# A Trainium2 expert stage: 64-row second blocks straight from the raw weights, a second output tensor for the last six blocks, and the final norm of all rows ahead of them

## The chip, the cores and the metric

The kernel runs on one core of a Trainium2 chip. The metric is the device time of the kernel in microseconds (us). Engines are named as in the profile: PE (TensorE) multiplies matrices, DVE (VectorE) and ACT (ScalarE) work on tiles, POOL (GpSimd) works on tiles and issues the indirect DMAs, SP (SyncE) issues most of the other DMAs.

## What is computed

A decoder block over S = 2048 rows of D = 1024 numbers, all in fp32: a norm, a projection, two attention mixers, a mixture of experts, a final norm. The change touches the last two. Cut to these, the reference is:

```python
# x: [2048, 1024] after the mixers; h = rms_norm(x, g)
grp = argmax(h @ w_group + b_group)              # one of 4 groups per row
top_v, top_i = top_k(e_logits_of_the_group, 2)   # 2 of its 8 experts
weight = p_grp * softmax(top_v)
# for each of the 4096 (row, expert) pairs:
y = (silu(h_row @ w_gate_e[e]) * (h_row @ w_up_e[e])) @ w_down_e[e]   # 1024 -> 256 -> 1024
x[row] += weight * y
out = rms_norm(x, norm_final_g)
```

There are 32 experts. How many rows each gets is known at run time only; with the reference's inputs it is 82 to 209 rows.

## The kernel before

One Python program writes the instructions of PE, DVE, ACT and POOL in an order that a planner (`Weave`) fixes beforehand: each piece of work is a generator that yields a time at which it can go on, each operation books a cost on its engine (`W.op`), and the piece that is ready first is written next. The engines then run their streams in that order and wait on semaphores. So an operation that waits holds up everything written behind it on its engine. SP's DMAs stand in one queue, in the order in which they were written, and at most eight of them are under way.

**Before the experts.** `route_setup` writes zero-weight entries into the four list tensors: 32 DMAs of 128 KB from the tile `padv`, on SP (L1407). They stand in the middle of the projection: on SP behind and ahead of them are the stores of q (L440), and behind these the loads of the next columns of the weights (`fraw`, L290). ACT evicts q from PSUM (L432) into tiles that the stores must have read before they are used again, and splits each weight column into a high and a low part (`apart`, L174 on ACT, L180 on DVE or POOL) for products in three matmuls (`mm3`, L187 to L189).

**Slots.** The experts are put in order of their row counts (experts 0 and 1 come first in any case). The 20 with the most rows get two blocks of 128 rows, the other 12 one: 52 slots, in the order of the list `SLOTS`; what is beyond is done by a loop at the end (L2254), which has nothing to do with these inputs. `lists` builds on DVE and PE (L2074) the table that says which row numbers belong to which slot. Then six generators run: `load` and `chunk` bring an expert's weights in six chunks of 512 KB, four of gate and up (L1915) and two of down (L1917), into a ring of four buffers `raw3`, and split them; a buffer is given back after its split. `fetch` gathers the slot's rows from `h2` (L1970, POOL, indirect). `turn` transposes them (L2108, eight transposes) and splits them. `enter` does gate and up (24 matmuls of 128x512), `act` silu and the product, `leave` the transposes of the result (L2162), its split, and down (12 matmuls), whose result is scaled on DVE and ACT (L2188, L2191) and added to the rows of `x2` in memory by an indirect store (`scatter`, L1977, POOL).

**The end.** `rest` first computes on DVE a table of what is left for the loop (L2217 to L2252, a dozen steps of up to 1x1024), reads its count (L2253), runs the loop, and then loads the 16 tiles of `x2` (L2305, SP), squares and sums each (L2311, ACT), computes the inverse roots in small DVE operations (L2313, `rsqrt`), scales (L2317, DVE) and stores (L2319, on ACT's queue).

## Time and profile before

| | before |
|---|---|
| median of three runs | 2665.09 us (2662.35 to 2671.33) |
| the profiled execution: its own time | 2665.63 us |
| its span in the trace | 2663.9 us |
| PE busy | 2469.3 us, 93% |
| DVE, ACT, POOL busy | 1470.3, 1070.2, 1169.7 us |
| DMA | 430.70 MB, mean 162 GB/s |
| expert stage, its slots | from about 2100 to 2610 us |

All rows of the trace are of that one execution, so its span and own time are what a sum is made against; the runs around it differ by a few microseconds. Busy shares are means over the whole span: the page's 93% hides that the stages have different limits, and the stretch at hand has to be read by itself. In the chain of waits each row is a piece of work that ended last at that point; what is not in the chain costs nothing as long as it stays out of it.

### The profile page before, as it was taken

To read this page: it belongs to the slowest core of one execution; us is meant where nothing else is said; L and a number is where in the kernel's file an instruction comes from. 1 tells how busy PE (TensorE), PEld (TensorE's weight loads), DVE (VectorE), ACT (ScalarE), POOL (GpSimd) and SP (SyncE) were. 2 spreads that over 40 slices of the span, in tenths; PEclk is the share of its full clock that TensorE was granted. 3 is DMA by queue.
4 is the path that set the end of the run, shared out by engine and by line. 5 is a ranking of instruction groups with operands and counts; after the bars stand their busy time and mean duration, and the time that the engine had idled before them with its cause. 6 is when DMAs were issued, how large, how long until landed. Compare 5 with 4: busy or idle time off the path is not lost.

```text
span 2663.9 us, 38518 instructions
## 1 busy us (share of the span) xinstructions
PE 2469.3 (93%) x13504; PEld 1928.7 (72%) x13504; DVE 1470.3 (55%) x3338; ACT 1070.2 (40%) x1674; POOL 1169.7 (44%) x931
## 2 busy tenths in 40 slices
PE   6999998989899899999999998999999899999991
PEld 5898886767566566677666664899888688888871
DVE  7402114757477666637776672422465566766666
ACT  5311113545333334344333333423332466666653
POOL 1012112323145556664566677444432356666650
PEclk9999998999999999999999998999999999999995
DMA  8613648676732242245322212865643479998877
GB/s 297 215 52 99 184 123 206 177 204 188 175 80 74 60 123 63 65 113 162 107 65 67 60 48 56 271 185 183 208 147 139 150 239 296 287 280 267 271 216 265
DMA packets 274682, 430.70 MB, mean 162 GB/s; under 512 B 52493, under 2 KB 184087, under 8 KB 270901
## 3 DMA queue, kind: packets, MB, share of 16 engines
q1 hardware_dynamic: 246967, 369.43, 46.0%
q0 software_dynamic: 16000, 33.63, 5.8%
q10 hardware_dynamic: 11520, 25.17, 2.5%
q8 instruction: 107, 1.75, 0.3%
q14 instruction: 88, 0.72, 0.1%
HBM read 317.18 MB, written 131.89 MB: 169 GB/s over the span
## 4 chain that ended last, share of the span: by engine, by line
PE 80%; DVE 7%; DMA 6%; POOL 3%; issue 2%; ACT 2%; SPq 1%; ACTq 0%; POOLq 0%; DVEq 0%
PE bank L321 21%; PE bank L187 10%; PE bank L189 10%; PE bank L188 10%; PE bank L1053 7%; PE bank L1001 4%; PE bank L1041 3%; PE bank L1044 3%; POOL zs L1062 2%; PE bank L1070 2%; PE bank L2108 2%; PE bank L1043 1%; PE bank L1029 1%; DMA qa<-q 1%; DMA gb<-gate 1%
## 5 line engine op out<-in xcount | busy, mean ns | idle before, releaser
L1046 ACT ACTIVATE p<-bank 128x512 f32<-128x512 f32 x458 | 266.2, 597 | 432.0 <-PE bank L1044 404.7
L180 POOL TENSOR_TENSOR fwl<-fraw,fwh 128x1024 fp32r<-128x1024 f32 x54 | 130.0, 2408 | 527.3 <-ACT fwh L174 497.9
L1062 POOL TENSOR_TENSOR zs<-zs,p 128x512 f32<-128x512 f32 x229 | 298.2, 1302 | 29.0 <-ACT p L1046 10.0
L1080 DVE RECIPROCAL rz<-bank 128x256 f32<-128x256 f32 x126 | 219.7, 1749 | 64.7 <-PE bank L1070 64.4
L321 PE MATMUL bank<-fhh,fwh 128*128 128x512 f32 x616 | 247.5, 402 | 4.1 <-ACT fwh L174 4.1
L321 PE MATMUL bank<-fhh,fwl 128*128 128x512 f32 x616 | 247.1, 401 | 1.7 <-POOL fwl L180 1.7
L321 PE MATMUL bank<-fhl,fwh 128*128 128x512 f32 x616 | 246.4, 400 | 0.0
L1053 PE MATMUL bank<-p,v 128*64 128x256 f32 x1704 | 234.5, 416 | 3.2 <-ACT p L1046 3.0
L174 ACT CAST wh<-raw 128x1024 fp32r<-128x1024 f32 x192 | 199.6, 1052 | 34.6 <-DMA raw<-in_w_gu_e_dram 22.7
L180 DVE TENSOR_TENSOR wl<-raw,wh 128x1024 fp32r<-128x1024 f32 x123 | 178.3, 1455 | 45.1 <-ACT wh L174 42.4
L180 POOL TENSOR_TENSOR wl<-raw,wh 128x1024 fp32r<-128x1024 f32 x69 | 167.3, 2425 | 81.7 <-ACT wh L174 81.2
L1044 PE MATMUL bank<-q,ka 128*128 128x512 f32 x426 | 199.6, 468 | 0.0
L1053 PEld LDWEIGHTS bank<-p,v 128*64 128x64 f32 x1704 | 124.7, 148 | 83.2 <-issue 22.7
L187 PE MATMUL bank<-wh,oh 128*128 128x512 f32 x416 | 172.4, 415 | 0.0
L1004 DVE TENSOR_REDUCE mx<-bank 128x1 f32<-128x512 f32 x192 | 128.2, 687 | 75.2 <-PE bank L1001 74.7
L1001 PE MATMUL bank<-kb,qa 96*128 96x512 f32 (+3 forms) x448 | 155.6, 378 | 9.3 <-DMA kb<-k 8.6
L189 PE MATMUL bank<-wh,ol 128*128 128x512 f32 x416 | 164.0, 394 | 0.0
L188 PE MATMUL bank<-wl,oh 128*128 128x512 f32 x416 | 163.3, 393 | 0.0
L1062 POOL TENSOR_TENSOR zs<-p 128x512 f32<-128x512 f32 x86 | 111.2, 1294 | 90.0 <-ACT p L1046 71.9
L1084 POOL TENSOR_TENSOR rz<-rz,gb 128x256 f32<-128x256 f32 x96 | 72.7, 758 | 175.8 <-DVE rz L1080 150.7
L1041 PE MATMUL bank<-qa,kb 97*128 97x512 f32 x362 | 148.7, 411 | 0.8 <-ACT qa L1031 0.7
L321 PEld LDWEIGHTS bank<-fhh,fwh 128*128 128x128 f32 x616 | 118.3, 192 | 30.9 <-ACT fwh L174 4.9
(490 smaller groups left out, 6091.5 us busy)
## 6 DMA issues: line engine op xcount, KB each, us to landing
raw<-in_w_gu_e_dram SPq DMA_DIRECT2D x128, 512.0 KB
fraw<-in_w_cols_dram SPq DMA_DIRECT2D x77, 512.0 KB
raw<-in_w_down_e_dram SPq DMA_DIRECT2D x64, 512.0 KB
xt<-in_x_dram SPq DMA_DIRECT2D x32, 512.0 KB
sg<-fo ACTq DMA_DIRECT2D x64, 256.0 KB
q<-q SPq DMA_DIRECT2D x64, 256.0 KB
sg<-sg SPq DMA_DIRECT2D x64, 256.0 KB
gb<-gate SPq DMA_DIRECT2D x64, 192.0 KB
```

The lines of the kernel that those rows point to most:

```text
L180: e.tensor_tensor(out=lo, in0=src, in1=hi.bitcast(F32), op=ALU.subtract)
L187: mm(out, lhsT=wh, rhs=xh, start=first, stop=False, **kw)
L188: mm(out, lhsT=wh, rhs=xl, start=False, stop=False, **kw)
L189: mm(out, lhsT=wl, rhs=xh, start=False, stop=last, **kw)
L321: K.T.matmul(ps, lhsT=w[:, k, :], rhs=self.H[ch][x][f][:, k % 4], start=k == 0 and j == 0, stop=k == 7 and j == 2)
L1001: T.matmul(ps[:, :w], lhsT=q1[0:rows, h, :], rhs=kb[0:rows, a:a + w], start=True, stop=True)
L1041: T.matmul(ps, lhsT=kb, rhs=q1, start=True, stop=False)
L1044: T.matmul(ps, lhsT=ka, rhs=q2, start=False, stop=True)
L1046: A.activation(p, ps, AF.Exp)
L1053: T.matmul(u[hp * 64:hp * 64 + 64, 0], lhsT=v, rhs=p[:, 2 * hp:2 * hp + 2, :], start=first, stop=last, skip_group_check=True)
L1062: e.tensor_tensor(out=out, in0=a, in1=b, op=ALU.add)
L1080: V.reciprocal(r, z)
```

## The change

**Half blocks.** Of the 20 experts with two blocks, the 15 in places 5 to 19 of the order now have a second block of at most 64 rows, a half block. Its rows are gathered as 64 rows, transposed into 64 columns and not split: ACT copies them, and the matmuls take fp32 on both sides, the weights straight from the raw chunks. 16 matmuls of 64x256 for gate and up write two groups of 64 columns into the two halves of a PSUM tile's partitions, 4 of 64x512 do down, each set in one unbroken piece (`enter_half`, `leave_half`). The result goes out in 128 pieces of 2 KB (`scatter_half`). The raw gate chunks of these experts go to a ring of their own (`fx`, four buffers `xf`), the two down chunks to `raw3`; all are given back when both their split and the half block have used them. The order of the experts is now in pairs, one other expert and one with a half block; the half block is done before the full one, but for the last expert.

**Table.** The steps of the table of what is left are a generator `table`, started as soon as the lists are there.

**z.** A second tensor `z` is zeroed by 16 DMAs behind the pads of the lists. The last six slots (`LATE`) add into z instead of x2.

**Final norm.** `finals` loads x2 once the other slots have been added, two tiles at a time, into buffers of `fx` and `raw3`, norms them and stores them (on SP's queue now). `once_more` then treats the rows of each of the six late slots: it gathers them from x2 and from z (POOL), adds (DVE), norms, and writes them to `out` by an indirect store; this comes after all 16 tiles have been stored.

**Setup.** `lists` has 16 more matmuls and two more DVE operations, `moe_setup` sets its table by 104 memsets instead of 16 and eight iotas.

```diff
+        zv = sc["z"].rearrange("(a p) (b n) -> a p b n", p=128, n=256)
+        for a in range(16):
+            nc.sync.dma_start(zv[a], pad[:, None, :].to_broadcast([128, 4, 256]))
...
-TWOS, ONES = 20, 12
-
-
+HALF = 64
+FULL, TWOS = 5, 20
+_halves, _others = list(range(FULL, TWOS)), list(range(2, FULL)) + list(range(TWOS, NE))
 ORDER = [(0, 2), (1, 2)]
-for _g in range(6):
-    ORDER += [(2 + 3 * _g, 2), (20 + 2 * _g, 1), (3 + 3 * _g, 2), (21 + 2 * _g, 1), (4 + 3 * _g, 2)]
+for _h, _o in zip(_halves, _others):
+    ORDER += [(_o, 2 if _o < FULL else 1), (_h, 2)]
 SLOTS = [(0, 0, 0), (1, 1, 0), (0, 0, 1), (1, 1, 1)]
-SLOTS += [(n, r, b) for n, (r, c) in enumerate(ORDER) for b in range(c) if n > 1]
+for _n, (_r, _c) in list(enumerate(ORDER))[2:]:
+    SLOTS += [(_n, _r, _b) for _b in ((1, 0) if FULL <= _r < TWOS - 1 else range(_c))]
 NS = len(SLOTS)
 
+LATE = 6
...
+        self.fx = K.keep("mf", bufs=4)
+        self.fR = Ring(4)
...
+                if c < 4 and is_half(r):
+                    self.fR.take()
+                    raw = self.fx.tile([128, 1024], F32, name="xf")
+                else:
+                    rawR.take()
+                    raw = K.raw.tile([128, 1024], F32, name="raw3")
                 self.chunk_load(raw, ws, c)
                 self.chunk(n, c, raw, W.dma(0.52))
 
...
+            if is_half(ORDER[n][0]):
+                self.raw_used(n, c, t)
+            else:
+                K.rawR.give(t)
...
+    def raw_used(self, n, c, t):
+        if (n, c) in self.half_used:
+            (self.fR if c < 4 else self.K.rawR).give(max(t, self.half_used.pop((n, c))))
+        else:
+            self.half_used[n, c] = t
...
+    def scatter_half(self, y, tk, to="x2"):
+        K = self.K
+        K.G.indirect_dma_start(out=K.sc[to].rearrange("s (c n) -> (s c) n", c=2),
+                               out_offset=bass.IndirectOffsetOnAxis(ap=tk, axis=0), in_=y, in_offset=None,
+                               bounds_check=2 * S - 1, oob_is_err=False, compute_op=ALU.add)
...
+                xt = K.pairs.tile([128, 8, 128], F32R, name=f"oh{s % 2}").bitcast(F32)[:, :, 0:HALF]
+                p8 = flat(K.bank(), 8, HALF)
+                for k in range(8):
+                    T.transpose(p8[:, k, :], xg[:, k * 128:(k + 1) * 128], K.ident[0:HALF, 0:HALF])
...
+    def enter_half(self, s, n):
+        K, W, guR, raws = self.K, self.K.W, self.guR, self.raws
+        yield lambda: NEVER if (s, 0) not in self.xts or (n, 3) not in raws or not self.xp else max(
+            self.xts[s, 0][1], raws[n, 3][1], guR.ready()) + HOP
+        guR.take()
+        gu = flat(K.bank(), 2, 128)
+        W.op("T", 0.2)
+        for k in range(8):
+            w = raws[n, k // 2][0].rearrange("p (k u f) -> p k u f", k=2, u=2)[:, k % 2]
+            for g in range(2):
+                K.T.matmul(gu[g * HALF:(g + 1) * HALF], lhsT=self.xts[s, 0][0][:, k], rhs=w[:, :, g * 128:g * 128 + 128],
+                           start=k == 0, stop=k == 7, skip_group_check=True)
+            t = W.op("T", 0.43)
+            if k % 2:
+                self.raw_used(n, k // 2, t)
...
+        for k in range(2):
+            for c in range(2):
+                T.matmul(ps[c * HALF:(c + 1) * HALF], lhsT=hh[:, k * HALF:(k + 1) * HALF],
+                         rhs=raws[n, 4 + k][0][:, c * 512:c * 512 + 512], start=k == 0, stop=k == 1,
+                         skip_group_check=True)
+            t = W.op("T", 0.86)
+            self.raw_used(n, 4 + k, t)
+        K.A.mul(out=y, in_=ps, mul=self.rows_of[s][2])
...
+    def put(self, y, s, yR):
+        W = self.K.W
+        to = "x2" if s < NS - LATE else "z"
+        if is_half(*SLOTS[s][1:]):
+            self.scatter_half(y, self.rows_of[s][3], to)
+        else:
+            self.scatter(y, self.rows_of[s][0], S if s > 1 else FIRST * 256, to)
+        self.scattered += 1
+        yR.give(W.op("D", 1.0, W.op("G", 1.04)) + 2.1)
+        if s >= NS - LATE:
+            self.late.append(self.rows_of[s][0])
+            self.once_more()
+    def once_more(self, end=False):
+        if self.stored < 16:
+            return
+        while len(self.late) > (0 if end else 1):
+            k = self.late.popleft()
+            self.turned.append((self.sum_rows(k), k))
+            if len(self.turned) > 1:
+                self.write_rows(*self.turned.popleft())
...
+    def sum_rows(self, k):
+        K, W, V = self.K, self.K.W, self.K.V
+        ss, rs = [K.sm.tile([128, 1], F32, name=f"{c}sa") for c in "sr"]
+        xs = [self.fx.tile([128, D], F32, name="xf") for _ in range(2)]
+        for xt, src in zip(xs, ("x2", "z")):
+            K.G.indirect_dma_start(out=xt, out_offset=None, in_=K.sc[src],
+                                   in_offset=bass.IndirectOffsetOnAxis(ap=k, axis=0), bounds_check=S - 1,
+                                   oob_is_err=False)
+            t = W.op("G", 1.04)
+        xt = xs[0]
+        def norm():
+            V.tensor_tensor(out=xt, in0=xt, in1=xs[1], op=ALU.add)
+            K.A.activation(self.junk, xt, AF.Square, accum_out=ss)
+            self.normed([xt], ss, rs, "a")
+            W.op("V", 4.4, W.op("A", 1.05, W.op("V", 1.23)))
...
+    def normed(self, xs, ss, rs, tag):
+        K, V = self.K, self.K.V
+        V.tensor_scalar(ss, ss, 1.0 / D, EPS, op0=ALU.mult, op1=ALU.add)
+        K.rsqrt(rs, ss, K.sm, tag)
+        for j, xt in enumerate(xs):
+            V.scalar_tensor_tensor(xt, xt, rs[:, j:j + 1], self.gb, op0=ALU.mult, op1=ALU.mult)
+    def finals(self):
+        K, W, A = self.K, self.K.W, self.K.A
+        yield lambda: 0.0 if self.scattered >= NS - LATE and self.tabled else NEVER
+        for n in range(8):
+            ring, pool, name = (self.fR, self.fx, "xf") if n % 4 < 2 else (K.rawR, K.raw, "raw3")
+            if len(ring.f) < 2:
+                yield lambda: 0.0 if len(ring.f) >= 2 else NEVER
+            ss, rs = [K.sm.tile([128, 2], F32, name=f"{c}sf") for c in "sr"]
+            xs, left = [], [2]
+            def norm(n=n, xs=xs, ss=ss, rs=rs, ring=ring):
+                self.normed(xs, ss, rs, "f")
+                W.op("V", 4.6)
+                for j, xt in enumerate(xs):
+                    tt = self.tiles[2 * n + j]
+                    K.dma(self.out[tt * 128:(tt + 1) * 128, :], xt)
+                    ring.give(W.dma(0.52))
+                self.stored += 2
+                self.once_more()
+            def square(j, xs=xs, ss=ss, left=left, norm=norm):
+                A.activation(self.junk, xs[j], AF.Square, accum_out=ss[:, j:j + 1])
+                t = W.op("A", 1.05)
+                left[0] -= 1
...
+            for j in range(2):
+                ring.take()
+                xs.append(pool.tile([128, D], F32, name=name))
+                K.dma(xs[j], K.sc["x2"][(2 * n + j) * 128:(2 * n + j + 1) * 128])
...
+        self.once_more(end=True)
         n_more = nc.values_load(tn[0:1, 0:1], min_val=0, max_val=32)
...
-        K.close_right()
-        cp = K.keep("fc")
-        xp = K.keep("fx", bufs=16)
-        sm = K.keep("fs", bufs=2)
-        xs = []
-        for t in range(16):
-            xs.append(xp.tile([128, D], F32, name="xf"))
-            dma(xs[t], sc["x2"][t * 128:t * 128 + 128])
-        t = 0
-        for n in (1, 2, 3, 3, 3, 2, 1, 1):
-            ss = sm.tile([128, n], F32, name=f"ssf{n}")
-            for j in range(n):
-                junk = cp.tile([128, D], BF, name="junkf")
-                A.activation(junk, xs[t + j], AF.Square, accum_out=ss[:, j:j + 1])
-            rs = sm.tile([128, n], F32, name=f"rsf{n}")
-            V.tensor_scalar(ss, ss, 1.0 / D, EPS, op0=ALU.mult, op1=ALU.add)
-            K.rsqrt(rs, ss, sm, f"f{n}")
-            for j in range(n):
-                xt = xs[t + j]
-                V.scalar_tensor_tensor(xt, xt, rs[:, j:j + 1], self.gb, op0=ALU.mult, op1=ALU.mult)
-                tt = self.tiles[t + j]
-                nc.scalar.dma_start(out[tt * 128:(tt + 1) * 128, :], xt)
-            t += n
+            self.scatter(y, k, to="z")
+            self.write_rows(self.sum_rows(k), k)
```

### Where instructions stand

SP in the projection, around the pads (`list` the lists, `padv` the tile they are written from, `q` and `sh`, `sl` the stored queries, `fraw` a weight column). Before:

```order
L1407 DMA list_125<-padv 128x256 x8
L1407 DMA list_126<-padv 128x256 x8
L1407 DMA list_127<-padv 128x256 x8
L1407 DMA list_128<-padv 128x256 x8
L440 DMA q_3_79<-sh 64x4x128
L440 DMA q_3_79<-sl 64x4x128
L440 DMA q_3_79<-sh 64x4x128
L440 DMA q_3_79<-sl 64x4x128
L290 DMA fraw<-in_w_cols_dram 128x1024
```

Now:

```order
L1409 DMA list_126<-padv 128x256 x8
L1409 DMA list_127<-padv 128x256 x8
L1409 DMA list_128<-padv 128x256 x8
L1409 DMA list_129<-padv 128x256 x8
L1412 DMA z<-padv 512x1x256 x16
L440 DMA q_3_79<-sh 64x4x128
L440 DMA q_3_79<-sl 64x4x128
L440 DMA q_3_79<-sh 64x4x128
L440 DMA q_3_79<-sl 64x4x128
L290 DMA fraw<-in_w_cols_dram 128x1024
```

The 16 DMAs to z stand between the pads and the next stores of q, and the load of the next weight column behind them.

DVE at the end of the last slot (`raw`, `lb`, `tfo`, `jb`, `tn`, `ti`, `cum` belong to the table, `hm` and `ym` to a slot, `ssf` and `rsf` to the final norm, `ssa` and `rsa` to a late block). Before:

```order
L2188 TENSOR_SCALAR ym<-bank,ws 128x512
L2243 TENSOR_REDUCE lb<-raw_25414 1x32
L2143 TENSOR_TENSOR hm<-bank,hm 128x256
L2247 SCALAR_TENSOR_TENSOR tfo<-eb,lb 1x32
L2248 TENSOR_SCALAR jb<-jb 1x32
L2252 CAST tn<-cum 1x1
L2249 TENSOR_TENSOR tfo<-tfo,jb 1x32
L2250 CAST ti<-tfo 1x32
L180 TENSOR_TENSOR hml<-bank,hmh 128x256
L2188 TENSOR_SCALAR ym<-bank,ws 128x512
L2253 TENSOR_LOAD tn
```

Now, and then where the eighth pair ends and the first late block begins:

```order
L180 TENSOR_TENSOR wl_25044<-raw_25041,wh_25043 128x1024
L2246 TENSOR_TENSOR hm<-bank,hm 128x256
L2246 TENSOR_TENSOR hm<-bank,hm 128x128
L180 TENSOR_TENSOR hml<-bank,hmh 128x256
L2294 TENSOR_SCALAR ym<-bank,ws 128x512
L2407 TENSOR_SCALAR ssf<-ssf 128x2
L205 TENSOR_SCALAR rsf<-ssf 128x2
L206 TENSOR_SCALAR rsf<-rsf 128x2
```

```order
L2410 SCALAR_TENSOR_TENSOR raw_25308<-raw_25308,rsf,gbf 128x1024
L2410 SCALAR_TENSOR_TENSOR raw_25310<-raw_25310,rsf,gbf 128x1024
L2382 TENSOR_TENSOR xf<-xf 128x1024
L2407 TENSOR_SCALAR ssa<-ssa 128x1
L205 TENSOR_SCALAR rsa<-ssa 128x1
```

The table has left this place. The first norm of two tiles stands right behind the last `ym` of the slots, the other seven pairs follow it without anything between, and the six late blocks follow these.

ACT at the same place (`junkf` the squares of a tile of x2, `hmh` the copy that the half block's down multiplies with). Now:

```order
L2243 ACTIVATE hm<-bank 128x128
L174 CAST hmh<-bank 128x256
L2297 ACTIVATE ym<-bank,ws 128x512
L2434 ACTIVATE junkf,ssf<-xf 128x1024
L2315 COPY hmh<-bank 128x128
L2434 ACTIVATE junkf,ssf<-xf 128x1024
L2336 ACTIVATE ym<-bank,ws_20427 128x512
```

The first square, which needs a loaded tile of x2, stands ahead of the last half block's copy (L2315); before, no operation of the final norm stood ahead of one of the slots.

## Rows read from the trace of the kernel before

**Rows 1.** The page: span, PE's busy time, one group of instructions (busy, mean ns).
```profile
span 2663.9 us, 38518 instructions
...
PE 2469.3 (93%) x13504; PEld 1928.7 (72%) x13504; DVE 1470.3 (55%) x3338; ACT 1070.2 (40%) x1674; POOL 1169.7 (44%) x931
...
L180 POOL TENSOR_TENSOR fwl<-fraw,fwh 128x1024 fp32r<-128x1024 f32 x54 | 130.0, 2408 | 527.3 <-ACT fwh L174 497.9
```

**Rows 2.** Windows: busy per engine (count), then PEclk, DMA share, GB/s.
```profile
2200.00:2250.00 50.00, 50.00 (x246) 41.24 (x245) 33.47 (x41) 33.76 (x48) 32.55 (x19) 1.00 0.95 303
...
2250.00:2300.00 50.00, 50.00 (x245) 41.31 (x244) 34.90 (x38) 32.96 (x47) 32.32 (x18) 1.00 0.96 279
...
2600.00:2664.00 64.00, 7.74 (x26) 5.24 (x24) 39.29 (x120) 20.51 (x36) 3.11 (x2) 0.57 0.73 271
```

**Rows 3.** Chain of waits in the expert stage: start us, us, what.
```profile
2349.69 0.87 PE bank L2108 x8
...
2350.56 0.23 PE bank L187
...
2359.11 0.87 PE bank L2108 x8
```

**Rows 4.** DMA from 2200 to 2590: packets, MB, share of 16 engines; issues, landing.
```profile
q1 hardware_dynamic: 22344, 81.33, 59.7%
...
q0 software_dynamic: 11379, 25.21, 30.2%
...
x<-ym,toks POOLq DMA_INDIRECT x42, 7.9
...
xg<-h,toks POOLq DMA_INDIRECT x38, 6.2
```

**Rows 5.** Timeline of PE: start us, us, engine, line, operation, tile, count.
```profile
1103.67 2.81 PE L1053 MATMUL bank<-p,v 128*64 128x256 f32 x24
```

**Rows 6.** Timeline of SP's DMA issues, the 32 pads.
```profile
267.30 16.58 SPq L1407 DMA_DIRECT2D list<-padv  x32
```

**Rows 7.** Timeline of ACT: eviction of q, weight split, later eviction.
```profile
287.88 0.60 ACT L432 ACTIVATE sh<-bank 128x512 fp32r<-128x512 f32 x1 [12.33 <-DMA q<-sh]
...
294.65 1.05 ACT L174 CAST fwh<-fraw 128x1024 fp32r<-128x1024 f32 x1
...
313.41 0.60 ACT L432 ACTIVATE sh<-bank 128x512 fp32r<-128x512 f32 x1 [4.89 <-PE bank L321]
```

**Rows 8.** Timeline of PE: the matmuls of the lists.
```profile
2121.25 0.91 PE L2074 MATMUL bank<-perm,raw 64*128 64x52 f32 x6
...
2122.51 1.38 PE L2074 MATMUL bank<-perm,raw 64*128 64x52 f32 x10 [0.35 <-DMA raw<-list]
```

**Rows 9.** Chain of waits, from the last slots to the end.
```profile
2586.88 1.23 DVE wl L180
...
2588.36 1.21 DVE raw L2220
...
2602.82 1.13 DVE lb L2243
...
2606.59 0.43 PE bank L188
...
2615.72 6.12 DMA xf<-x
```

**Rows 10.** Timeline of DVE: first and last operation of a norm of two rows.
```profile
2623.10 0.17 DVE L2313 TENSOR_SCALAR ssf<-ssf 128x2 f32<-128x2 f32 x1
...
2625.49 2.48 DVE L2317 SCALAR_TENSOR_TENSOR xf<-xf,rsf,gbf 128x1024 f32<-128x1024 f32 x2
```

**Rows 11.** Groups after 2600 us: busy us, mean ns, idle before.
```profile
L2317 DVE SCALAR_TENSOR_TENSOR xf<-xf,rsf,gbf 128x1024 f32<-128x1024 f32 x16 | 19.8, 1282 | 0.3
...
L2311 ACT ACTIVATE junkf<-xf 128x1024 bf16<-128x1024 f32 x16 | 16.9, 1056 | 26.2 <-DMA xf<-x 11.3 <-DVE xf L2317 8.0 <-DVE rsf L205 6.5
```

**Rows 12.** Groups of POOL from 2100 to 2620: the indirect stores.
```profile
L1977 POOL DMA_INDIRECT x<-ym,toks x50 | 83.9, 1679 | 103.0 <-ACT ym L2191 25.8 <-ACT hm L2140 21.2 <-DVE ol L180 17.2
```

194 lines of the change are left out of this document (154 added, 40 removed).

## The prediction

> **What bounds the kernel now.** The page comes first: TensorE (PE) is busy for 93% of a span of 2663.9 us [rows 1]. That is a mean over stages, so I went to the windows of the expert stage. From 2200 to 2300 us PE is busy without a gap, while the DMA engines are already at 0.95 and 0.96 of their time, moving 303 and 279 GB/s [rows 2]: PE is the bound there, with the transfers close behind. After 2600 us PE works for 7.74 us only [rows 2]: a tail of small VectorE (DVE) work. The chain of waits gives the price of a full slot of 128 rows: its eight transposes start at 2349.69 and again at 2359.11, 9.4 us apart, with matmuls 0.23 us apart [rows 3]. The DMA view says what a byte costs: SP's queue (q1) moved 81.33 MB in 59.7% of 390 us, which is 2.86 us per MB at full use of the engines; POOL's indirect queue (q0) 25.21 MB in 30.2%, 4.67 us per MB [rows 4].
>
> **The change, part by part.** The sum is made against the profiled execution: span 2663.9 us, own time 2665.63 us; the median of the runs, 2665.09 us, is 0.5 us from it.
>
> **1. Half blocks on PE.** Fifteen second blocks become half blocks. The nearest row to their matmuls (64 columns of the array, fp32, two groups of columns) is the attention's: 24 records of 128x256 in 2.81 us, 0.117 us each, and a matmul of the program leaves two records, so 0.23 us for one [rows 5]. Sixteen for gate and up are 3.75 us, four of twice the width 1.87 us; with some 0.9 us of transposes a half slot is 6.5 us against 9.4. Were PE alone the bound, 15 x 2.9 = 43.5 us would go.
>
> **2. What is late next: the weights.** A half block computes from the raw chunks, so no byte of weights goes away. A usual pair of experts (12 of the 15) has three slots, 28.2 us on PE before and 25.3 after. It loads 12 chunks, 6.29 MB, 18.0 us at 2.86 us per MB; it gathers and scatters about 239 rows (3230 rows stand in the 27 experts ranked 5 to 31 of the reference's inputs), 1.96 MB, 9.1 us at 4.67. That is 27.1 us of full DMA use, and 28.3 at the best share seen, 0.96 [rows 2]. DMA is then the bound: I take 27.6 us, near full use since PE no longer holds the buffers, so 12 x 0.6 = 7 us. In the three pairs whose other expert has two full blocks PE stays the bound (34.7 us for 37.6): 9 us. **Expert stage: -16 us**, bounds -8 (pairs of 28.3 us) and -43.5 (PE alone). The gate chunks of the half block lie in a ring of their own and are loaded ahead; its two down chunks hold two of the four old buffers until PE has used them. That is a rival below. The splits of the half blocks' own rows on ACT and DVE fall away; they lay beside PE already and count nothing.
>
> Here the Trainium skill speaks for a better outcome: its page "DMA: Bandwidth & Descriptors", section "Bandwidth", gives 425 GB/s for a 16 MB stream of one core. By it a pair's 8.25 MB would be an estimated 19.4 us and PE would stay the bound. The trace disagrees so far: its windows at 0.95 and 0.96 reach 303 and 279 GB/s.
>
> **3. Zeroing z.** Sixteen DMAs of 512 KB stand on SP's queue right behind the 32 pads. Those 32 (128 KB each, 4.19 MB) take 16.58 us [rows 6], so z's 8.39 MB take 33 us at that rate, 27.7 at 303 GB/s, 24 at q1's full rate. Behind them wait the stores of q. ACT's eviction at 287.88 had already waited 12.33 us for such a store behind the pads, and the split of the next weight column stands behind it on ACT, at 294.65 [rows 7]; with POOL's part (2.41 us [rows 1]) it was ready at about 298.2, and PE began that column at about 313.4 (the eviction of that time [rows 7]). So 15 us of cover, against a delay of 24 to 33: PE idles 9 to 18 us. I take 11, and 2 more for the clock: behind PE's gap before 2604 us the matmuls stand 0.43 us apart instead of 0.23 for some dozen [rows 9], the level of 1.2 GHz, and the granted clock of that window is 0.57 on average [rows 2]. **+13 us**, bounds 0 (if the cover is larger) and +20.
>
> **4. Lists.** PE's 16 matmuls for the lists take 0.91 and 1.38 us [rows 8], and the change adds 16 matmuls and two small DVE operations to a path on which PE then waits for the first gather. **+2 us** (0 to 4). The first steps of the table and the memsets lie under idle DVE time: nothing; without that cover about 10 us, the price the table now has in the tail.
>
> **5. The table's dozen steps** stand in the last slots now: 1.21 us at 2588.36 to 1.13 at 2602.82, nine of them 10.5 us of the chain, and PE's last matmuls behind them at 0.43 us [rows 9]. They move to the start of the expert stage, where DVE has room. **-7 us** (-4 to -12). One thing comes with it: SP's read of the count moves up between two loads of the fourth expert's chunks and waits for the table and for all DMAs in flight; the loads behind it come later by one drain, about one landing. That pair is bound by PE: **+1** (0 to 8).
>
> **6. The tail.** On DVE all eight pairs of final norms stand behind the last operation of the last slot, and the six late sums behind these; the words of the change are true of loads alone. Before, from the last matmul (about 2610.0) to the end is 53.9 us. After:
> - The first x2 tile in the new ring needs a buffer that the last half's gate-up frees, and ACT squares it ahead of the copy that the last half's down waits for. Load 6.12 us [rows 9], square 1.16, and so on: the norms begin some 9 us after that gate-up, 3.5 us after PE would have ended.
> - A pair is 2.4 us of small operations and 2.48 us of scaling [rows 10], 39 us for eight, bound below. In that time 14 loads and 16 stores (15.7 MB) share the queue, 52 us at 303 GB/s from the gate-up on, some 43 after the norms' start. I take 43.
> - A late sum is an add (1.23 us, as DVE's operation of that size [rows 9]), a square (1.06 [rows 11]), 2.1 us of small operations and a scaling of 1.28 [rows 11], with handovers about 6 us. Before it lie two gathers and behind it a write by POOL (a store's issue 1.68 us [rows 12]; landing 6.2 and 7.9 [rows 4]), two sums in four buffers: of the six, the later four wait for buffers. 36 us if nothing waits, some 46 if each turn of two takes 16; I take 37.
> - The last write with the end: 5.5 us.
> Together 3.5 + 43 + 37 + 5.5 = 89 us against 53.9: **+35 us**, bounds +25 (39, 36, no wait at the start) and +46.
>
> **Sum:** -16 + 13 + 2 - 7 + 1 + 35 = +28. 2665.6 + 28 = **2694 us**, slower by 1.1%. About 0.3%, 8 us, is what a measurement of this kernel can tell from no change.
>
> **The rivals.**
> - **The transfers keep up (faster).** If POOL's transfers too run at q1's full rate, a pair's 8.25 MB take 23.6 us and PE stays the bound of every pair: -43.5 instead of -16. z then takes 24 us, so +8 with its clock; the norms are DVE's 39 us and the sums 36, the tail +27 (without waits for buffers). -43.5 + 8 + 2 - 7 + 0 + 27 = -13: 2652 us. For it: PE takes what the transfers now spare, and the 303 GB/s of one window were reached at a share below 1. Against it: q0's price per byte in the whole stretch [rows 4], and the other window's 279 GB/s at the same share. It decides if a pair takes under 25.8 us. 0.18. (The page of the Trainium skill named above would have it so.)
> - **Half the way (no change).** Pairs of 26.5 us, a gain of 29; z +9, lists +2, table -7, tail +27: +2, 2668 us. 0.14.
> - **The held chunks starve the half blocks.** After a half's down, eight chunks (4.19 MB) must land within some 13 us of PE's work, 320 GB/s, more than any row shows. At 279 GB/s that is 15 us, and a split (1.05 us on ACT [rows 7], 1.23 on DVE [rows 9]) behind it, so 17.3 for 13.1 us and about 30 us a pair: instead of -16 the stage gives +13. 2723 us. 0.11.
> - **z stops PE for nearly all of its writing:** 33 us at the pads' rate with 11 us of cover, so 22 and 2 for the clock, 11 more than forecast: 2705 us. 0.12.
>
> **How the numbers follow.** The forecast keeps 0.45. Slower by over 8 us: 0.45 + 0.12 + 0.11 = 0.68; within: 0.14; faster: 0.18. The range goes from 2652 (half of the first rival left out) to 2716 (most of the starved case left out, and the upper ends of tail and z). The likeliest case alone is 2678 to 2710.
>
> **What would show it.** Half gate-ups on PE of 3.75 us in a piece. In the windows of the expert stage a DMA share of 0.97 or more with PE short of full, waiting for splits and raw chunks, pairs 27 to 28 us apart. A gap on PE near 313 us. No table operation near the end; from the last matmul to the end 80 to 95 us, in which DVE does eight pairs, then six sums. Wrong, if pairs are 25 us apart, if the norms or sums overlap the last slots' matmuls, or if the tail is under 75 us.

## The result, and the profile after

| | before | after |
|---|---|---|
| median of four runs | 2665.52 us (2662.35 to 2671.33) | 2738.23 us (2734.75 to 2738.82) |
| span of the profiled execution | 2663.9 us | 2736.0 us |
| end of the routing (last transposes) | 2100.5 | 2113.4 |
| first gathered rows on PE after the lists | 2130.2 | 2143.7 |
| last matmul ends | 2609.8 | 2639.1 |
| from there to the end | 54.1 | 96.9 |

The changed kernel takes 1.0268 times as long (95% interval 1.0248 to 1.0287), 72.7 us more. The forecast was 2694, the range ended at 2716. The table splits the 72.1 us of the spans: 12.9 up to the end of the routing, 0.6 at the lists, 15.7 in the slots (479.7 us before, 495.4 now), 42.8 behind the last matmul. The page of the changed kernel begins (compare [rows 1]):

```profile
span 2736.0 us, 38876 instructions
...
PE 2457.7 (90%) x13581; PEld 1865.9 (68%) x13581; DVE 1466.1 (54%) x3436; ACT 1071.2 (39%) x1686; POOL 1187.1 (43%) x939
...
PE 70%; DMA 8%; issue 6%; DVE 6%; POOL 5%; ACT 2%; SPq 1%; ACTq 0%; POOLq 0%; DVEq 0%
```

PE has 11.6 us less to do and idles 84 us more. The last line is the chain by engine: 70% of it is still PE, the rest is spread.

**z.** SP's queue, ACT and PE in the projection (compare [rows 6, 7]; in brackets the idle time before the instruction and what ended it):

```profile
268.40 17.64 SPq L1409 DMA_DIRECT2D list<-padv  x32
286.09 21.26 SPq L1412 DMA_DIRECT2D z<-padv  x16
...
314.56 0.60 ACT L432 ACTIVATE sh<-bank 128x512 fp32r<-128x512 f32 x1 [37.83 <-DMA q<-sh]
...
320.46 1.04 ACT L174 CAST fwh<-fraw 128x1024 fp32r<-128x1024 f32 x1
...
321.55 0.79 PE L321 MATMUL bank<-hh,fwh 128*128 128x512 f32 x1 [6.48 <-ACT fwh L174]
...
323.99 0.80 PE L321 MATMUL bank<-hh,fwl 128*128 128x512 f32 x1 [1.22 <-POOL fwl L180]
```

ACT's wait for the store of q has grown from 12.33 to 37.83 us, the split behind it starts at 320.46 instead of 294.65, and PE idles 7.7 us in two pieces; after them its matmuls stand some 0.43 us apart for a while, not 0.23.

**The pairs.** From the third half block on, the half blocks' gate-ups are 28.2 to 30.3 us apart in eleven turns, 29.5 on average. Windows of four pairs (busy per engine, then PEclk, DMA share, GB/s; compare [rows 2]), PE's longest waits in ten pairs (us in all, times, longest), and the DMA view of that stretch:

```profile
2316.29:2346.48 30.19, 27.67 (x143) 19.51 (x141) 16.22 (x19) 18.57 (x27) 17.81 (x11) 0.94 0.83 278
2376.55:2405.21 28.66, 25.98 (x142) 18.68 (x141) 16.11 (x19) 18.56 (x27) 17.52 (x11) 1.00 0.86 287
2435.07:2463.23 28.16, 25.99 (x142) 18.69 (x141) 16.28 (x19) 18.50 (x27) 18.61 (x11) 1.00 0.87 296
2463.23:2493.55 30.32, 27.69 (x143) 19.45 (x142) 16.12 (x19) 18.57 (x27) 17.95 (x11) 0.94 0.81 265
```

```profile
PE bank L2268 <- DVE hm L2246: 21.4, 10, 3.1
PE bank L188 <- DVE wl L180: 3.7, 9, 0.4
```

```profile
DMA  9964999399939994999399959974999399949983
GB/s 358 384 158 77 353 414 290 57 329 410 324 54 311 409 335 82 349 412 296 51 348 411 303 112 363 412 222 67 330 414 291 47 325 408 310 74 365 411 254 60
...
q1 hardware_dynamic: 16935, 61.67, 54.8%
q0 software_dynamic: 7952, 19.03, 27.7%
```

PE's own work in a pair is 26.0 us; in every pair it also waits some 2 us for `hm`, the full block's product on DVE, and about half of the pairs lose 1.7 us more to the clock (PE busy 27.7, clock 0.94). With some 0.4 us of waits for splits (`wl`) this comes to 29.3 us on average. The DMA engines are not full: in each pair they reach 384 to 414 GB/s in a slice of 7.4 us and then fall to 47 to 112. The rows round one such wait, on ACT, DVE and PE:

```profile
2443.20 1.98 ACT L174 CAST wh<-xf 128x1024 fp32r<-128x1024 f32 x2
2445.09 0.38 ACT L2243 ACTIVATE hm<-bank 128x256 f32<-128x256 f32 x1
```

```profile
2444.27 2.36 DVE L180 TENSOR_TENSOR wl<-xf,wh 128x1024 fp32r<-128x1024 f32 x2 [0.61 <-ACT wh L174]
2446.55 0.42 DVE L2246 TENSOR_TENSOR hm<-bank,hm 128x256 f32<-128x256 f32 x1
```

```profile
2389.38 3.67 PE L2231 MATMUL bank<-xf,oh 128*64 128x256 f32 x32
...
2417.55 5.36 PE L2231 MATMUL bank<-xf,oh 128*64 128x256 f32 x32
...
2447.03 0.44 PE L2268 MATMUL bank<-ident,hm 128*128 128x128 f32 x2 [1.76 <-DVE hm L2246]
```

Two splits of the next chunks stand ahead of the silu on ACT and of the product on DVE, and PE has nothing else written there. The two half gate-ups are the same 16 matmuls (32 records) at the two levels of the clock.

The two turns before these, whose other expert has two full blocks, took 39.4 and 41.4 us. In the first of them the half block waited for its chunks (SP's issues of them, then PE):

```profile
2161.06 0.87 SPq L1935 DMA_DIRECT2D xf<-in_w_gu_e_dram  x2
...
2190.24 1.20 SPq L1935 DMA_DIRECT2D xf<-in_w_gu_e_dram  x2
```

```profile
2195.07 1.08 PE L2231 MATMUL bank<-xf,oh 128*64 128x256 f32 x8 [4.01 <-DMA xf<-in_w_gu_e_dram]
```

The early table works in two of the four buffers `xf` until about 2196, so two of the first half block's four loads went out only when PE had used the other two, at 2190. In the second turn PE waited 3.3 us for a split on POOL, and the granted clock was 0.92 on average.

**The end.** Windows after the last matmul, and rows of DVE and POOL (compare [rows 10, 11]):

```profile
2639.00:2684.00 45.00, 0.05 (x2) 0.00 (x0) 34.68 (x108) 16.70 (x29) 7.84 (x6) 0.55 0.96 323
2684.00:2736.00 52.00, 0.00 (x0) 0.00 (x0) 25.01 (x72) 6.89 (x12) 17.16 (x14) 0.50 0.28 93
```

```profile
2638.14 0.17 DVE L2407 TENSOR_SCALAR ssf<-ssf 128x2 f32<-128x2 f32 x1 [0.85 <-ACT junkf L2434]
...
2679.60 2.48 DVE L2410 SCALAR_TENSOR_TENSOR raw<-raw,rsf,gbf 128x1024 f32<-128x1024 f32 x2
2684.55 1.23 DVE L2382 TENSOR_TENSOR xf<-xf 128x1024 f32<-128x1024 f32 x1 [2.47 <-issue]
...
2690.29 1.22 DVE L2382 TENSOR_TENSOR xf<-xf 128x1024 f32<-128x1024 f32 x1
...
2699.60 1.23 DVE L2382 TENSOR_TENSOR xf<-xf 128x1024 f32<-128x1024 f32 x1 [3.48 <-DMA xf<-z,toks]
...
2724.83 1.28 DVE L2410 SCALAR_TENSOR_TENSOR xf<-xf,rsa,gbf 128x1024 f32<-128x1024 f32 x1
```

```profile
2674.62 1.44 POOL L2375 DMA_INDIRECT xf<-x,toks  x1 [25.30 <-DMA raw<-x]
...
2726.39 1.00 POOL L2395 DMA_INDIRECT out_dram<-xf,toks  x1 [3.99 <-DVEq L2531]
```

The norms begin when PE ends and take 44 us, at a DMA share of 0.96; the six sums follow one another for another 42, at 0.28; the last write and the end are 9.6.

### The profile page after: what moved, and what is told of

Its sections match the earlier page's. It is cut to its first block, busy times and chain, and to the rows that moved or that the text cites. A ratio compares the mean times of both kernels' runs of the same rounds, so it can differ in the third digit from the quotient of the medians.

```text
span 2736.0 us, 38876 instructions
## 1 busy us (share of the span) xinstructions
PE 2457.7 (90%) x13581; PEld 1865.9 (68%) x13581; DVE 1466.1 (54%) x3436; ACT 1071.2 (39%) x1686; POOL 1187.1 (43%) x939
## 3 DMA queue, kind: packets, MB, share of 16 engines
q8 instruction: 108, 1.77, 0.3%
## 4 chain that ended last, share of the span: by engine, by line
PE 70%; DMA 8%; issue 6%; DVE 6%; POOL 5%; ACT 2%; SPq 1%; ACTq 0%; POOLq 0%; DVEq 0%
PE bank L321 19%; PE bank L187 8%; PE bank L188 8%; PE bank L189 8%; PE bank L1055 7%; PE bank L1003 4%; PE bank L1043 3%; PE bank L1046 3%; POOL zs L1064 2%; PE bank L2231 2%; PE bank L1072 2%; DMA xf<-in_w_gu_e_dram 2%; PE bank L1045 1%; POOL wl L180 1%; PE bank L1031 1%
## 5 line engine op out<-in xcount | busy, mean ns | idle before, releaser
L180 DVE TENSOR_TENSOR wl<-raw,wh 128x1024 fp32r<-128x1024 f32 x91 | 133.3, 1496 | 29.7 <-ACT wh L174 27.1
L174 ACT CAST wh<-raw 128x1024 fp32r<-128x1024 f32 x132 | 136.8, 1052 | 9.2 <-DMA raw<-in_w_down_e_dram 7.0
L321 PEld LDWEIGHTS bank<-fhh,fwl 128*128 128x128 f32 x616 | 117.2, 190 | 27.4 <-issue 3.5
L321 PEld LDWEIGHTS bank<-fhl,fwh 128*128 128x128 f32 x616 | 117.6, 191 | 25.2 <-issue 3.1
L321 PE MATMUL bank<-hh,fwh 128*128 128x512 f32 x312 | 125.4, 402 | 6.5 <-ACT fwh L174 6.5
L188 PE MATMUL bank<-wl,oh 128*128 128x512 f32 x296 | 119.5, 404 | 8.8 <-DVE wl L180 5.5
```

The costliest lines, as they stand in the source:

```text
L180: e.tensor_tensor(out=lo, in0=src, in1=hi.bitcast(F32), op=ALU.subtract)
L188: mm(out, lhsT=wh, rhs=xl, start=False, stop=False, **kw)
L321: K.T.matmul(ps, lhsT=w[:, k, :], rhs=self.H[ch][x][f][:, k % 4], start=k == 0 and j == 0, stop=k == 7 and j == 2)
```

## The experiments

In each, "slots" is the time from the first gathered rows (behind the lists) to the last matmul, "tail" what follows, "pairs" the mean of the eleven turns from the third half gate-up to the fourteenth, and the kernel before was timed on the same chip beside it (medians 2658 to 2661 us there).

### The parts alone

**e1, zeroing z alone:** the kernel before with the three lines that create and zero z.

> The kernel before with only the 16 DMAs added that zero z (z is then not used). Theory: the DMAs hold up the stores of q, ACT's split of the next weight column and so PE: +13 us (9 to 16), about 2678 us, with one gap on PE near 322 us of 6 to 8 us and a stretch at the lower clock behind it. Rival (the gap is made up for later, because PE is not the bound behind it): within 3 us of the kernel before.

Measured: 2668.89 us against 2658.25, ratio 1.0039 (1.0027 to 1.0050), +10.6 us. PE's gap is there as in the changed kernel:

```profile
320.65 0.80 PE L321 MATMUL bank<-hh,fwh 128*128 128x512 f32 x1 [6.63 <-ACT fwh L174]
```

So z costs 10.6 us by itself.

**e2, half blocks alone:** the change without z and with the ending of before; the early table stays.

```diff
-LATE = 6
+LATE = 0
...
-        for n, th in enumerate((self.fetch(), self.leave(), self.turn(), self.enter(), self.finals())):
+        for n, th in enumerate((self.fetch(), self.leave(), self.turn(), self.enter())):
```

> The changed kernel without z and without its new ending: half blocks, the new order of experts and the early table, then the ending of the kernel before (all 16 tiles of x2 after the last slot, stores on ACT's queue). Theory: the expert stage itself got 16 us longer in the changed kernel (pairs of about 29.6 us), and the ending costs 54 us as before: 2681 us (2674 to 2688). Rival (the stage got longer only because the loads of x2 and the stores to z in its last pairs disturb it): pairs of 27 to 28 us and 2650 us or less.

Measured: 2685.27 us, ratio 1.0105 (1.0077 to 1.0132), +27 us, slots 489.0, pairs 29.2, 22.0 us of waits for `hm`. The half blocks, meant to spare PE work, are slower by themselves.

**e3, z and the new ending alone:** the change with no half expert, in the order of before.

```diff
-FULL, TWOS = 5, 20
+FULL, TWOS = 20, 20
```

> The changed kernel without half blocks: the 52 full slots in the order of the kernel before, with the early table, z, the norms in pairs and the six late blocks. Theory: the ending costs 43 us more, z 13, the table's steps 7 less: about 2715 us (2705 to 2722), 95 to 100 us from PE's last matmul to the end. Rival (the long ending is made by the last pair of half blocks, which frees the buffers late): 70 to 80 us from the last matmul to the end and about 2690 us.

Measured: 2725.78 us, ratio 1.0239 (1.0213 to 1.0266), +67.5 us: in the spans 16 up to the first gathered rows (z alone gave 10.6 in the time), 40 in the tail (94.1 us), 9 in the slots (489.1, with 9.6 us of waits for `hm`). The parts don't add up to the whole: 27 and 67.5 are 95, the change cost 73. What the two share (the early table is in both) was not followed further.

### The ending

**e17, no late blocks:** all blocks go to x2, the pairs of norms follow, nothing is summed again; z is still zeroed.

```diff
-LATE = 6
+LATE = 0
```

> The changed kernel with no late blocks: all blocks are added into x2, the norms of all sixteen tiles follow the last slot in pairs, and no rows are summed again; z is still set to zero. Theory (the six sums add some 50 us behind norms that cannot begin before the last slot's store, so the new ending loses by its sums): the tail falls from 97 to 58 to 66 us, time 2698 to 2710 us, ratio 1.014 to 1.02. Rival (the pairwise norms through two rings are themselves the long part): the tail stays over 75 us, time over 2715 us.

Measured: 2701.49 us, ratio 1.0168 (1.0146 to 1.0190), slots 493.4, tail 65.0, as the theory said. The six sums cost the changed kernel 32 us of tail. The norms begin when the last slot ends (2638.14 above), so the second tensor buys no overlap here. The tail is still 11 us longer than before's 54.1; that was not followed.

**e5, z zeroed later,** among the routing's work, from the gather tiles.

```diff
+    def zeros(self, xs):
+        K, W = self.K, self.K.W
+        for a in range(16):
+            at = W.t["T"] + 7.0
+            yield lambda: at
+            K.dma(K.sc["z"][a * 128:(a + 1) * 128], xs[a % 2])
+            W.dma(0.52)
```

> The changed kernel with z zeroed later: 16 DMAs of 512 KB from a zeroed tile, one every 7 us or so at about 1890 to 2010 us, where no store of q waits behind them. Theory: the gap on PE near 320 us goes and with it the 10 us that the zeroing alone cost: about 2728 us, 8 to 13 us faster than the changed kernel. Rival (the same bytes are paid wherever they are written, because the loads and stores of the merge stage then wait for them): the gap reappears after 1890 us and the time stays within 3 us of 2738.

Measured: 2736.56 us, ratio 1.0286 (1.0258 to 1.0314). Neither expectation holds. The routing ends at 2098.3, so z's gap is gone, but the slots take 503.0, with 15.7 us of waits for splits on POOL (3.3 in the changed kernel): the gain is lost again there. Why was not followed.

### What holds a pair at 29 us

**e4, the half block first:** PE gets something to do during the wait for `hm`, by writing the half gate-up ahead of the full block's transposes.

```diff
-            yield lambda: max(self.hs[0][1] + HOP, thR.ready(), hR.ready()) if self.hs else NEVER
+            first = s + 1 if s + 1 < NS and is_half(*SLOTS[s + 1][1:]) else s
+            yield lambda: (max(self.hs[0][1] + HOP, thR.ready(), hR.ready())
+                           if self.hs and first in self.entered else NEVER)
```

> The changed kernel with one rule added to the order: the transposes of a full block's result (L2268) are written only when the half block that follows has its gate-up written, so PE does the half block's 16 matmuls while ACT and DVE make that result. Theory: PE's wait of 2.1 us before these transposes and the half-clock stretches behind it are what makes a pair 29.6 us; pairs of 26 to 27 us, 30 to 36 us faster than the changed kernel: 2702 to 2708 us. Rival (the loads bound the pair, since the held down chunks leave two buffers; the wait only shows there): pairs stay at 28 to 30 us, within 10 us of 2738.

Measured: 2769.79 us, ratio 1.0418 (1.0393 to 1.0444), slots 532.4, pairs 32.2: slower than theory and rival. The wait for `hm` went down to 2.3 us in all, and another took its place (PE's waits from 2285 to 2560):

```profile
PE bank L188 <- POOL wl L180: 33.2, 8, 5.1
```

These splits stand on POOL behind an adding store that itself waits 6 to 9 us for the store before it:

```profile
2419.77 1.58 POOL L2020 DMA_INDIRECT x<-ym,row2s  x1 [9.46 <-DMA x<-ym,toks]
...
2422.76 4.66 POOL L180 TENSOR_TENSOR wl<-raw,wh 128x1024 fp32r<-128x1024 f32 x2
```

The theory that one wait was the loss fell.

**e9, e4 without splits on POOL** (ACT and DVE do them all):

```diff
-        K.W.later(t, lambda: K.apart(hi, lo, raw, t, 1024, done, pool_ok=True))
+        K.W.later(t, lambda: K.apart(hi, lo, raw, t, 1024, done))
```

> The changed kernel with the half block's gate-up ahead of the full block's transposes, and with no split of an expert's weights on POOL (DVE does all). Theory: in the run with that order alone, POOL's store of a half block waited for the landing of the store before it, and the split of a weight that PE needs stood behind it on POOL; without splits on POOL that wait of 4 us a pair goes: pairs of 26 to 28 us and 2700 to 2720 us. Rival (DVE becomes what POOL was: its splits stand ahead of the products that PE waits for): pairs of 30 us or more, 2740 us or more.

Measured: 2724.95 us, ratio 1.024 (1.0204 to 1.0276), slots 484.0, 11 less than the changed kernel; pairs 28.7, in turn about 26 and 31 long, short of the theory. PE now waits 19.2 us for gathers in the slots.

**e8, a ring of their own for all six raw chunks of a half expert,** else as e2:

```diff
-        self.fx = K.keep("mf", bufs=4)
-        self.fR = Ring(4)
+        self.fx = K.keep("mf", bufs=6)
+        self.fR = Ring(6)
...
-                if c < 4 and is_half(r):
+                if is_half(r):
```

> Half blocks with the ending of the kernel before and without z, as the second run, with all six raw chunks of a half expert in the ring of their own (six buffers), so that the four old buffers are given back after their split. Theory (held buffers): SP's loads no longer come in two bursts, pairs go from 29.5 to 26 to 28 us and the time to 2640 to 2665 us. Rival (PE's wait for the product of the full block and the half-clock stretch behind it are set by the order on PE, ACT and DVE, not by the loads): pairs stay at 29 to 30 us, 2678 to 2690 us.

Measured: 2689.85 us, ratio 1.0103 (1.0071 to 1.0135), pairs 30.2 and uneven (22 to 37): no better than e2. The held chunks alone are not the bound.

**e10, e2 with the half block first and no splits on POOL.**

> Half blocks with the ending of the kernel before and without z, the half block's gate-up first, and no split of an expert's weights on POOL. Theory: pairs of 26 to 28 us instead of 29.5, so about 20 to 30 us faster than the run with half blocks alone: 2655 to 2667 us, no slower than the kernel before. Rival (DVE's queue): pairs of 30 us or more and 2690 us or more.

Measured: 2673.22 us, ratio 1.0048 (1.0032 to 1.0064), 12 us better than e2 and short of the theory; pairs 28.7, in turn about 26 and 31. POOL, then PE:

```profile
2433.17 1.84 POOL L2011 DMA_INDIRECT x<-ym,toks  x1 [2.97 <-DVE ym L2293]
2443.00 1.58 POOL L2017 DMA_INDIRECT x<-ym,row2s  x1 [7.99 <-DMA x<-ym,toks]
2444.89 1.07 POOL L2004 DMA_INDIRECT xg<-h,toks  x1 [0.31 <-PE bank L189]
```

```profile
2453.02 1.62 PE L2185 MATMUL bank<-ident,xg 128*128 128x128 f32 x8 [2.15 <-DMA xg<-h,toks]
```

A store that adds into x2 waits 7.99 us until the one before it has landed, and the gather that PE needs next stands behind it. The program waits there. The Trainium skill's page "DMA: Bandwidth & Descriptors", section "Rules for kernel authors", says that an accumulating DMA beside another access of the same bytes can lose one of the writes, and to wait for the earlier one's semaphore. No run here left the wait out.

**e11, e10 with the half blocks' stores sent to z,** which nothing adds to the output: the half blocks' part of it is left out.

```diff
-            self.scatter_half(y, self.rows_of[s][3], to)
+            self.scatter_half(y, self.rows_of[s][3], "z")
```

> The run with half blocks alone, the half block first and no split on POOL, with the half blocks' results stored into z and never added to x2: their part of the output is left out. Theory: what bounds a pair there is that POOL's adding stores to x2 wait for one another's landing (8 us) and hold up the gathers behind them; with one store of three on another tensor, PE's 18 us of waits for gathers go and pairs are 26 to 27 us: 2640 to 2655 us. Rival (the gathers are late for lack of a buffer, or the transfers are slow): no change, 2668 to 2678 us.

Measured: 2664.97 us, ratio 1.0012 (0.9998 to 1.0025), some 10 us better than e10 by the ratios, between theory and rival; pairs 28.3 and even. PE's waits for gathers fell from 18.0 to 3.0 us in the stage, and from 2285 to 2560 this stands in their place:

```profile
PE bank L2228 <- DMA xf<-in_w_gu_e_dram: 13.7, 29, 1.9
```

**e12, e13, e14, the stores' landing in the planner:** it books 9 us for the landing of each adding store, in e10 (e12), in e2 (e13), and in e2 with the half block first (e14).

```diff
-            W.later(t, lambda y=y, s=s: self.put(y, s, yR))
+            self.later_put(t, y, s, yR)
...
+    def later_put(self, t, y, s, yR):
+        t = max(t, self.land)
+        self.land = t + 9.0
+        self.K.W.later(t, lambda: self.put(y, s, yR))
```

> The run with half blocks alone, the half block first and no split on POOL, with the planner told that a store can go out only 9 us after the one before, so that it writes gathers ahead of a store that would wait. Theory (the store's wait holds up the gathers): pairs of 26 to 27.5 us, 2645 to 2660 us, faster than the kernel before or level with it. Rival (the stores themselves bound the pair, three landings of 9 us): pairs stay at 28 to 29 us, 2668 to 2676 us.

> Half blocks with the ending of the kernel before and without z, in the changed kernel's own order on PE and with splits on POOL, with the planner told of the store's landing as in the run before. Theory: in this order the store waits little (1 us a pair), and what costs is PE's wait of 2 us for the full block's product and the half-clock stretch behind it: no change, 2680 to 2690 us. Rival (the store's wait was behind this too): 2665 us or less.

> Half blocks with the ending of the kernel before and without z, the half block's gate-up first, splits on POOL allowed, and the planner told of the store's landing. Theory: the 41 us that PE waited for splits behind stores on POOL in the run with the half block first go for the most part: 2655 to 2675 us, against about 2715 for that order without it. Rival (POOL is simply full: its splits, stores and gathers together bound the pair): 2690 us or more.

Measured: 2715.05 us (ratio 1.0209, interval 1.0173 to 1.0245), 2705.64 (1.0157, 1.0126 to 1.0188) and 2751.72 (1.0330, 1.0302 to 1.0358); slots 518, 511 and 561. e12 and e13 are slower than the kernels they start from, by 42 and 20 us (43 and 14 by the ratios); the one that e14 starts from was not run. Neither the theory nor the rival of e12 and e13 allowed for that, and e14 lies far beyond its theory. All three have 28 to 50 us of waits for `hm`. Telling the planner of a wait doesn't take it away; why the new order was so much worse was not followed.

**e15, all but the stores:** e8's ring, half block first, no splits on POOL.

> The kernel before with the half blocks alone (before's ending, no z), and with three things at once: all six raw chunks of a half expert in a ring of their own, the half block's gate-up ahead of the full block's transposes, and no weight split on POOL. Theory (several loops hold a pair at 28 to 30 us, each of them enough, and byte rate none of them): the stretched loads of e10's successor e11 (20.8 us of waits on xf) shrink with the own ring, but the adding stores on POOL stay in the loop of the gathers, so pairs stay at 28 to 28.5 us, slots 479 to 484 us, time 2658 to 2672 us with the kernel before at 2660. Rival (the held chunks and the splits were the whole of it): pairs 26 to 27 us, slots under 470 us, time under 2650 us.

Measured: 2664.17 us, ratio 1.0020 (1.0004 to 1.0037), slots 471.5, pairs 28.5: the time as in the theory, the slots 8 us shorter. PE waits for no load in the slots; what is left between 2280 and 2560 begins with

```profile
PE bank L2184 <- DMA xg<-h,toks: 18.5, 5, 5.3
```

and has 1.0 us at most in any other row.

**e16, e15 with the half blocks' stores sent to z,** never added, so their part of the output is left out.

> The kernel of e15 with the half blocks' stores sent to z instead of x2; they are never added to the output, so the half blocks' part of it is left out. Theory: with splits, held chunks and the chain of adding stores out of the way at once, nothing but PE's own 26 us is left: pairs 26 to 27.3 us, slots 452 to 470 us, time 2630 to 2650 us, faster than the kernel before. Rival (bytes after all: 103 MB at the mean rate of the stretch bound a pair): pairs 28 us or more, as in e11, with PE waiting for DMA xf, time 2658 us or more.

Measured: 2637.77 us, ratio 0.9929 (0.9903 to 0.9956), slots 451.5, pairs 26.7, as the theory said. Windows of the stage:

```profile
2300.00:2400.00 100.00, 97.17 (x543) 70.61 (x542) 73.44 (x87) 67.93 (x102) 38.65 (x24) 1.00 0.91 303
2400.00:2500.00 100.00, 99.14 (x547) 72.14 (x546) 73.99 (x87) 70.46 (x104) 37.47 (x23) 1.00 0.94 318
```

PE is nearly full again (97 and 99%), at pairs close to its own 26 us, and the DMA engines move 318 GB/s at a share of 0.94. With the half block first and no splits on POOL, the held chunks kept a pair at 28.3 us (e11) and the gathers behind adding stores at 28.5 (e15), each without the other; only with both gone too does PE's saving show. Splits on POOL as the only one left were not tried; what they cost stands in e4 against e9, 32.2 and 28.7 us a pair. Nor was the changed kernel's order (the half block second, with its wait for `hm`) tried with the other three gone, so whether that cure is needed too is not shown.

### A kernel that keeps the gain

**e18 and e19, gathers ahead of the stores:** e15, output whole, with one (e18) or two (e19) more gather buffers, so that POOL issues a gather one or two slots earlier. Room comes from loading the final norm's weights in the ending, and in e19 from one buffer of the half experts' ring. Of e18:

```diff
-        self.gb = self.cp.tile([128, D], F32, name="gbf")
...
+        self.xg2 = K.keep("mxh", bufs=1)
...
-        xg = self.xg.tile([128, D], F32, name="xg")[0:tk.shape[0]]
+        xg = (self.xg2.tile([128, D], F32, name="xh") if s % 3 == 2 else
+              self.xg.tile([128, D], F32, name="xg"))[0:tk.shape[0]]
...
+            if s == 2:
+                xgR.give(0.0)
```

> The kernel of e15 (before's ending, half blocks with a ring of their own, half block first, no splits on POOL, every store added into x2) with one gather buffer more, so that POOL issues a slot's gather one slot earlier and it no longer stands behind the adding store that it needs least; the final norm's weights are loaded in the ending to make room. Theory (in e15 only PE's 18.5 us of waits for gathers behind waiting stores stand between 28.7 and 26.2 us a pair): pairs 26.5 to 27.7 us, slots 455 to 466 us, time 2640 to 2656 us, at or below the kernel before at 2660. Rival (the stores themselves, each waiting for the one before, are too slow for a pair, and y's buffers then hold the slots): pairs 28 us or more with PE's waits moved to hm or hmh, time 2658 us or more.

> The kernel of e18 with two more gather buffers instead of one, the second at the price of one of the six buffers of the half experts' ring (the last raw chunk goes back to the shared ring). Theory: gathers are then early enough that PE waits for them under 4 us in all; pairs 26.2 to 27.4 us, time 2636 to 2652 us, unless the chunk in the shared ring holds up loads again (PE's wait for DMA xf over 10 us, pairs 28 us, as in e11). Rival (stores are the bound): no better than e15, 2660 us or more.

Measured: e18 2653.78 us against 2658.50, ratio 0.9978 (0.9965 to 0.9991), slots 465.2, pairs 27.6, with 12.4 us of waits for `hm` left in the slots; e19 2650.30, ratio 0.9965 (0.9952 to 0.9979), slots 453.4, pairs 26.7. Both as in their theories. PE's waits in e19 from 2285 to 2560, all of them:

```profile
PE bank L2233 <- DMA xf<-in_w_gu_e_dram: 6.0, 18, 1.9
PE bank L188 <- DVE wl L180: 0.8, 2, 0.4
```

Every store is still there, and where it stands right behind another it still waits for that one:

```profile
2428.89 1.57 POOL L2019 DMA_INDIRECT x<-ym,row2s  x1 [8.33 <-DMA x<-ym,toks]
```

PE no longer waits for a gather there, so the wait costs nothing that shows. e19 is 8 us below the kernel before and, by their ratios, 3% or some 80 us below the change; of these some 43 lie between the change and e2, that is in z and the new ending, which e19 leaves out.

## Why the prediction was wrong

The direction was right, the size was not: 2738 against 2694, outside the range.

1. **Half blocks on PE: right.** Forecast 25.3 us of PE's work in a pair, measured 26.0; a half gate-up 3.67 us (forecast 3.75) at full clock. In about half of the pairs it took 5.2 to 5.4, which the forecast didn't have.
2. **"DMA is then the bound: I take 27.6 us": this step failed.** Pairs took 29.5 us while the DMA engines stood at 0.81 to 0.87, where the forecast wanted 0.97. The price per MB that it rests on is not fixed: from the DMA view above q1 costs 2.62 us per MB in the changed kernel (54.8% of 295 us for 61.67 MB) and q0 4.29, so a pair's bytes come to 24.9 us of full use, not 27.1, less than PE's 26. e16 settles it: as many bytes loaded, gathered and stored in pairs of 26.7 us, and e19 does it with the output whole. Slices of the changed kernel reach 414 GB/s. The Trainium skill's page "DMA: Bandwidth & Descriptors", section "Bandwidth", gives 425 GB/s for 16 MB on one core. The slices are nearer to that than the 303 GB/s of the window that the prediction held against it. What held the pairs was the order of work on ACT, DVE and POOL, engines that are busy for 53 to 66% of a pair's time (in the four windows) and that the forecast left out: in the changed kernel PE's wait of 2.1 us a pair for the full block's product, with a split ahead of it on DVE (in the rows above the silu ends at 2445.47 and the product begins at 2446.55), and the half-clock stretches behind that wait (0.8 on average). With these shortened, e4 to e16 uncovered the next: splits and gathers behind a store that waits, and held chunks. The other half of the term failed as well: "PE stays the bound" at 34.7 us in pairs with two full blocks, where the two such turns of above took 39.4 and 41.4. In the slots the forecast's terms (-16, table -7, SP's read +1) come to -22, the trace has +15.7: some 21 of the difference lie in the eleven usual turns, 11 in these two.
3. **z: right.** +13 forecast, +12.9 up to the end of the routing, +10.6 alone in e1. PE's gap of 7.7 us is close to the forecast's lower end of 9.
4. **Lists:** +2 forecast, +0.6 measured.
5. **The table** has left the end, as forecast: the last half's down waits 0.5 us. Its 7 us can't be seen by themselves in slots that became longer. That its first steps cost nothing was wrong: they hold two buffers of the half blocks' chunks, for which PE waited 4.0 us. SP's read of the count waited 5.2 us for the table (+1 forecast for what that costs; what it costs PE can't be told apart here).
6. **The tail: right in its order, short in its size.** +35 forecast, +42.8 measured. The norms took 44 us (43), from PE's end on (the 3.5 us at the start weren't there). The sums took 42 with 2.5 ahead of them (37): two of them take 15 us, near the 16 that the text named as the case of waiting buffers. The last write and the end took 9.6 (5.5).

Of the 44 us that were missing, 38 are in the slots and 8 in the tail; z and the lists were 1.5 too high.

**The rivals.** "The held chunks starve the half blocks" had the price (30 us a pair, 2723 us) but not the mechanism: e8 gave these chunks buffers of their own, and pairs stayed at 30.2. It was one of several loops, not the only one. "The transfers keep up" had the mechanism right (a pair under 25.8 us of transfers, 24.9 in the changed kernel; PE the bound) for a kernel in which nothing else stands in the way, e16 or e19; its ending, too, lost more than it said.

## What to carry to other kernels

When work is taken off the engine that is full, look at every in-order engine that feeds it, however idle on average: count for one turn what stands ahead of the next product, split or gather, waits included, and take the longest such loop as the new bound. A turn with several loops of nearly the same length shows no gain until all of them are shortened, so try the cures together once before dropping them one by one. An instruction that must wait (a store that adds into a tensor another has just added to) is best placed behind what others need soon, by one or two more buffers for what stood behind it. And work that is moved to an idle place takes its buffers along: ask who waits for them there.

## What the runs showed of the hardware

- An indirect store that adds into a tensor, right behind another one, waits here for the landing of the first: 7.99 us in e10, 8.33 in e19, 9.46 in e4, with a median landing of 7.9 before [rows 4]. The wait is the program's.
- The share of the DMA engines' time is no measure of what is left: 0.95 went with 303 GB/s and 0.96 with 279 before [rows 2], 0.94 with 318 in e16, and single slices of the changed kernel reached 414.
- The clock halves for a stretch in some turns and not in others: half gate-ups of 5.36 and of 3.67 us both stand behind gaps of PE of about 2 us (1.77 us before the one at 2417.55, 2.27 before the one at 2389.38), so the gap's length alone doesn't tell which. In e16, almost without gaps, the granted clock was 1.00 throughout the two windows.
